# Rotating queries and keys through ScalarE copies, and attention maxima in the projections' PSUM banks, in a two-layer hybrid block

## The chip, the core and the metric

The kernel runs on one core of one Trainium2 chip. The metric is device time in microseconds; the kernel before takes 3040.97 us (median of three runs, 3040.70 to 3048.51). A core has TensorE (PE, with its weight loads listed apart as PEld), VectorE (DVE), ScalarE (ACT), GpSimd (POOL), SyncE (SP) and DMA queues. Each engine executes its own instructions in the order of the program; semaphores order them across engines. Matmuls write to PSUM, 8 banks of 512 fp32 columns per partition; the other engines read the results from there.

## The reference, cut to what matters

Two layers over 512 latent tokens `x` and 256 context tokens `xc`, model width 1024, all in fp32:

```
for l in 0, 1:
    hx, hc = modulated RMS norms of x and xc
    conv, qkv, o, i/f gates, aq, ak, av, branch gates = split(h @ w_in)
    conv_x  = conv branch (GLU, width-31 depthwise conv, layer norm, swish, projection)
    mlstm_x = 4 heads of 256, chunkwise scan forwards and backwards, context first
    q = rope(rms(aq) * q_norm_w);  k = rope(rms(ak) * k_norm_w)    # 8 heads of 64, 2 of keys
    attn_x  = softmax(q @ [k_ctx, k_x]) @ [v_ctx, v_x]
    x = x + g1 * ((gated sum of the three) @ w_out)
    x = x + g2 * conv_ffn(norm(x))
    # layer 0 does the same for xc (its queries see context keys alone, and no rope)
rope(x) = [x1*c - x2*s, x1*s + x2*c]     # halves of 32 channels, c and s per position
```

The norm's factor is one number per token and head, and the rotation mixes only channels of one token and head, so rotation and factor may be applied in either order.

## The kernel before

Channels lie on partitions and tokens on the free axis: a tile is 128 channels by 512 latent and, in layer 0, 256 context tokens (`tq` is 768 in layer 0 and 512 in layer 1). Every fp32 operand is split into a high and a low part, and a product is three matmuls: hl by wh, hh by wl, hh by wh (L717).

Weights stream in units of four 128x128 blocks (256 KB). `Weights.load` issues the DMA of a unit from SP; `Weights.split` makes the high part on ACT (L215) and the low part by a subtraction (L217), on POOL, or on DVE for odd units while `shared` is set; it is set in the output projections and in the down projection at the end of layer 0, where odd units arrive in tiles P of other use. `take` hands out blocks; at the start of a unit it has split `SPLITS` = 2 units ahead.

The order of the work is made when the program is built. A `Filler` holds a queue of projections and runs them step by step (a step is three matmuls of 512 columns, or six, of 512 and 256, in layer 0), and after each step it ticks chains: generators that issue some instructions and then `yield` a number of ticks until the next. Chains touched here are `mgates` (the i/f gates: a serial row of DVE and ACT instructions, L840 to L960, whose table `t` goes to PE at L904), `qk_norm` (L1026: square, norm sums through PE, factor, rotation), `prepare` (L1453: for each of 8 heads, scores' row maxima by blocks of 128 queries; matmuls L1472 and L1479, maxima L1473 and L1481, transposition L1489 into an extra row of the query tile) and the mLSTM heads. The latter follow the tables `HEADS` and `HEADS1`: `2:S0 16:R0` starts the scores of group 0 (three pairs of chunk blocks, L1111, `score_gap` steps apart) at step 2, and its normalisation at step 16; the denominators are summed on DVE at L1131 and go to PE at L584.

PSUM has three pools: `sm` (2 tiles of 512 columns), `pv` (2 of 512) and `mm`, the projections' own, which has 2 tiles of 1024 in layer 0 and 4 of 512 in layer 1. Of the two `pv` tiles one holds the running weighted sum of attention (L1565, read out by L1573) during a head, so the maxima of the next head go through the other, one after the other.

## Time and profile before

| | |
|---|---|
| median of three runs | 3040.97 us (3040.70 to 3048.51) |
| the profiled execution | 3040.4 us, of which the span from first to last instruction 3038.6 us |
| mean granted TensorE clock | 0.973 of full speed |
| PE busy | 2827.8 us, 93% of the span |
| DVE, ACT, POOL busy | 1817.7, 1156.8, 1146.6 us |

The profile is one execution. Its page gives busy time by engine; the view of waits lists, for a stretch, which line of PE waited for which instruction of another engine; the view by windows gives the busy time of each engine in a stretch with the clock granted to TensorE (1 is 2.4 GHz and 0.5 is 1.2 GHz); the timeline gives instructions one by one. Stages by time from the span's start: gates of layer 0 at 61 to 105 us, attention of layer 0 at 740 to 1000, its output projection from 1100, gates of layer 1 at 1805 to 1850, the mLSTM heads of layer 1 at 1850 to 2260, attention at 2300 to 2520, output projection at 2596 to 2700.

### The profile page before, as it was taken

How to read it: one execution, taken by the hardware profiler on the slowest of the kernel's cores; microseconds unless marked ns; L12 is line 12 of the kernel's file. 1: busy time of each engine (PE TensorE's matmuls, PEld its weight loads, DVE VectorE, ACT ScalarE, POOL GpSimd, SP SyncE). 2: the span in 40 equal slices, each digit the busy share in tenths (PEclk: the TensorE clock that was granted, in tenths of full speed). 3: DMA queues.
4: the chain of work that ended last, by engine and by line, in shares of the span. 5: the costliest groups of instructions: out<-in, count | busy, mean ns of one | idle time of the engine just before them, and what ended most of it. 6: DMA issues, size and time to landing. Idle time of an engine off the chain costs nothing. (4 is left out here: it accounts for less than half of the span.)

```text
span 3038.6 us, 42068 instructions
## 1 busy us (share of the span) xinstructions
PE 2827.8 (93%) x15970; PEld 2381.7 (78%) x15970; DVE 1817.7 (60%) x2521; ACT 1156.8 (38%) x2122; POOL 1146.6 (38%) x931
## 2 busy tenths in 40 slices
PE   7999999899889998999999988999889889899999
PEld 4888888787667887888888867887767567778887
DVE  4376787825554336876765555777774763554444
ACT  5224334324345334322322253433444344443333
POOL 2233343224244334333333333333344345444444
PEclk9999999999999999999999999999999999999999
DMA  6454334221010242333333232333322112423333
GB/s 242 133 149 69 58 67 68 49 60 52 28 28 29 63 130 93 115 101 118 118 115 115 75 102 68 65 75 67 65 75 69 39 38 76 154 87 100 93 96 110
DMA packets 156681, 262.47 MB, mean 86 GB/s; under 512 B 17784, under 2 KB 37624, under 8 KB 156480
## 3 DMA queue, kind: packets, MB, share of 16 engines
q1 hardware_dynamic: 142560, 249.67, 28.0%
q10 hardware_dynamic: 13920, 10.12, 3.1%
q8 instruction: 126, 2.06, 0.3%
q14 instruction: 75, 0.61, 0.1%
HBM read 247.05 MB, written 5.46 MB: 83 GB/s over the span
## 5 line engine op out<-in xcount | busy, mean ns | idle before, releaser
L217 POOL TENSOR_TENSOR wl<-raw,wh 128x512 fp32r<-128x512 f32 x659 | 904.6, 1379 | 1507.6 <-ACT wh L215 1461.0
L717 PE MATMUL mm<-hh,wh 128*128 128x512 f32 (+1 forms) x2672 | 963.6, 361 | 17.0 <-DVE big L1619 7.1
L717 PE MATMUL mm<-hh,wl 128*128 128x512 f32 (+1 forms) x2672 | 949.1, 355 | 10.7 <-POOL wl L217 10.6
L717 PE MATMUL mm<-hl,wh 128*128 128x512 f32 (+1 forms) x2672 | 954.4, 357 | 2.1 <-POOL hl L372 1.2
L215 ACT ACTIVATE wh<-raw 128x512 fp32r<-128x512 f32 x662 | 411.2, 625 | 580.2 <-PE mm L717 358.4
L717 PEld LDWEIGHTS mm<-hh,wh 128*128 128x128 f32 x2672 | 512.4, 192 | 113.3 <-issue 29.6
L717 PEld LDWEIGHTS mm<-hh,wl 128*128 128x128 f32 x2672 | 510.4, 191 | 89.4 <-POOL wl L217 15.5
L717 PEld LDWEIGHTS mm<-hl,wh 128*128 128x128 f32 x2672 | 512.3, 192 | 71.4 <-POOL hl L372 1.8
L717 PE MATMUL mm<-C,wh 128*128 128x512 f32 (+1 forms) x1168 | 410.2, 351 | 0.3 <-DVE C L372 0.3
L717 PE MATMUL mm<-B,wh 128*128 128x512 f32 (+1 forms) x976 | 344.4, 353 | 24.4 <-DVE big L1619 11.8
L717 PE MATMUL mm<-B,wl 128*128 128x512 f32 (+1 forms) x976 | 342.5, 351 | 9.2 <-POOL wl L217 8.8
L993 DVE SCALAR_TENSOR_TENSOR AC<-G,par,AC 128x783 f32<-128x783 f32 (+1 forms) x240 | 261.1, 1088 | 3.6
L717 PEld LDWEIGHTS mm<-C,wh 128*128 128x128 f32 x1168 | 226.6, 194 | 28.3 <-DVE C L372 0.5
L717 PEld LDWEIGHTS mm<-B,wh 128*128 128x128 f32 x976 | 190.1, 195 | 53.7 <-ACT wh L215 14.5
L717 PEld LDWEIGHTS mm<-B,wl 128*128 128x128 f32 x976 | 189.4, 194 | 37.4 <-POOL wl L217 14.2
L1669 DVE SCALAR_TENSOR_TENSOR AC<-mm,par,AC 128x511 f32<-128x511 f32 (+1 forms) x132 | 86.7, 656 | 199.0 <-ACT AC L1667 199.0
L1619 DVE SCALAR_TENSOR_TENSOR big<-mm,mod,big 128x512 f32<-128x512 f32 (+1 forms) x144 | 91.1, 657 | 116.3 <-PE mm L717 116.1
L1667 ACT ACTIVATE AC<-mm,par 128x768 f32<-128x768 f32 (+1 forms) x88 | 77.4, 880 | 145.0 <-PE mm L717 144.8
L372 POOL TENSOR_TENSOR P<-t,P 128x512 fp32r<-128x512 f32 (+1 forms) x64 | 75.1, 1175 | 139.2 <-ACT t L1550 111.2
L527 DVE SCALAR_TENSOR_TENSOR P<-C,cs,P 128x512 f32<-128x512 f32 x112 | 116.5, 1072 | 0.9 <-DMA C<-aw 0.9
L1565 PE MATMUL pv<-P,B 128*128 128x512 f32 (+1 forms) x336 | 94.6, 387 | 12.1 <-DVE G L1573 5.2
L1097 ACT ACTIVATE C<-rb,bias 128x128 f32<-128x128 f32 x312 | 96.4, 390 | 21.4 <-DMA rb<-rows 11.2
(282 smaller groups left out, 3726.5 us busy)
## 6 DMA issues: line engine op xcount, KB each, us to landing
raw<-ws SPq DMA_DIRECT2D x662, 256.0 KB, 2.6
C<-aw SPq DMA_DIRECT2D x104, 256.0 KB, 3.0
big<-aw SPq DMA_DIRECT2D x64, 256.0 KB, 4.7
P<-ws SPq DMA_DIRECT2D x30, 256.0 KB, 2.9
big<-xt SPq DMA_DIRECT2D x16, 384.0 KB, 6.3
rb<-rows ACTq DMA_DIRECT2D x40, 128.0 KB, 4.2
den<-rd ACTq DMA_DIRECT2D x40, 64.0 KB, 6.3
den<-rd SPq DMA_DIRECT2D x40, 64.0 KB, 6.3
```

The lines of the kernel that those rows point to most:

```text
L215: self.nc.scalar.activation(out=hi, in_=raw, func=AF.Copy)
L217: eng.tensor_tensor(out=lo, in0=raw, in1=hi.bitcast(F32), op=ALU.subtract)
L372: (eng or dve).tensor_tensor(out=out, in0=src, in1=hi.bitcast(F32), op=ALU.subtract)
L527: dve.scalar_tensor_tensor(out=a_, in0=r_, scalar=cs[:, k, q:q + 1], in1=a_, op0=ALU.mult, op1=ALU.add)
L717: pe.matmul(ps[:, o:o + n], w[w_], h[h_][:, so:so + n], start=(k == 0 and i == 0 and o % 512 == 0), stop=(k == n_k - 1 and i == 2), skip_g ...
L993: dve.scalar_tensor_tensor(out=a, in0=t[:, j:j + cw], scalar=par(l, "cw", w0 + j), in1=a, op0=ALU.mult, op1=ALU.add)
L1097: act.activation(out=t[:, off + x * 128:off + x * 128 + 128], in_=rb[:, c0:c0 + 128], func=AF.Exp, bias=bcol(dr, h, key, qb))
L1565: pe.matmul(o_[:, 0:n_q], vblock(b, a_)[:, 64 * v_:64 * v_ + 128], b_[:, 0:n_q], start=(ki == 0 and x == 0), stop=(last and x == 2))
L1619: dve.scalar_tensor_tensor(out=xs[m][:, o:o + n], in0=ps[:, po:po + n], scalar=gain[:, m, s:s + 1], in1=xs[m][:, o:o + n], op0=ALU.mult, o ...
L1667: act.activation(out=t[:, 0:tq], in_=ps[:, 0:tq], func=AF.Identity, scale=fw(1), bias=fb)
L1669: dve.scalar_tensor_tensor(out=t[:, o + 1:o + n], in0=ps[:, o:o + n - 1], scalar=fw(0), in1=t[:, o + 1:o + n], op0=ALU.mult, op1=ALU.add)
```

## The change

It has four parts. First, `qk_norm` rotates before the norm's factor is known: one tick after the projection's eviction, four copies on ACT swap the halves (32 partitions by 512 columns each), then three DVE products of 128x512 follow; the factor is multiplied in last. Before, the swap and the product with the sine were four DVE products of 32x512 after the factor. Second, `prepare` takes its latent maxima in `mm` tiles: in layer 0 two blocks of 512 columns or four of 256 per tile, and one reduction for the tile; in layer 1 the six reductions stay, one tile each. Context queries stay in `pv`. Third, while `shared` is set the parts of odd units go to tiles AC instead of the ring of `wh` and `wl`, and splits run one unit further ahead. Fourth, `mgates` yields more ticks, 33 in all instead of 21, and the tables move: in layer 1 the first o gate of head 0 runs before the gates' end, `score_gap` is 4 instead of 5 there, R0 stands at 18 instead of 16, S1 at 25 instead of 22, R1 at 41 instead of 39.

```diff
-HEADS1 = [["c o0 o1 q v", "2:S0 4:D1 16:R0 22:S1 39:R1 40:V0 61:V1 61:D*"]] * 3 +     [["c o0 o1 b b x0", "2:S0 4:D1 15:R0 21:S1 35:R1 38:V0 51:V1 51:s"]]
+HEADS1 = [["c o1 q v", "2:S0 4:D1 18:R0 25:S1 41:R1 42:V0 60:V1 60:D*"]] + [["c o0 o1 q v", "2:S0 4:D1 18:R0 25:S1 41:R1 42:V0 61:V1 61:D*"]] * 2 +     [["c o0 o1 b b x0", "2:S0 4:D1 15:R0 21:S1 35:R1 38:V0 51:V1 51:s"]]
...
-       dict(COMMON, partial=3, heads=HEADS1, early=1, first_max=8, send_gap=3, norm_gap=11, first="Q g K v",
+       dict(COMMON, partial=3, score_gap=4, heads=HEADS1, early=1, first_max=8, send_gap=3, norm_gap=11, first="Q g K o v",
...
-            hi = self.pool.tile([128, UNIT * 128], F32R, tag="wh", name=f"wh{self.l}_{u}")
-            lo = self.pool.tile([128, UNIT * 128], F32R, tag="wl", name=f"wl{self.l}_{u}")
+            if self.shared and u % 2:
+                hi, lo = self.room(), self.room()
+            else:
+                hi = self.pool.tile([128, UNIT * 128], F32R, tag="wh", name=f"wh{self.l}_{u}")
+                lo = self.pool.tile([128, UNIT * 128], F32R, tag="wl", name=f"wl{self.l}_{u}")
...
-            self.split(u + SPLITS + 1)
+            self.split(u + SPLITS + 1 + self.shared)
...
-                yield 5
+                yield 6
                 dve.tensor_scalar(out=u[R, :], in0=e[R, :], scalar1=1.0, scalar2=None, op0=ALU.add)

                 dve.scalar_tensor_tensor(out=e[R, :], in0=u[R, :], scalar=1.0, in1=e[R, :], op0=ALU.subtract,
                                          op1=ALU.subtract)
-                yield 1
+                yield 2
                 act.activation(out=ln[R, :], in_=u[R, :], func=AF.Ln)
                 act.activation(out=u[R, :], in_=ln[R, :], func=AF.Exp, scale=-1.0)
                 dve.tensor_tensor(out=e[R, :], in0=e[R, :], in1=u[R, :], op=ALU.mult)
+                yield 3
+                dve.tensor_tensor(out=ln[R, :], in0=ln[R, :], in1=e[R, :], op=ALU.subtract)
                 yield 2
-                dve.tensor_tensor(out=ln[R, :], in0=ln[R, :], in1=e[R, :], op=ALU.subtract)
-                yield 1
                 for P_, nat, sc in dirs:
                     dve.scalar_tensor_tensor(out=lf[P_, sc], in0=z[P_, nat], scalar=0.0, in1=ln[P_, nat], op0=ALU.min,
                                              op1=ALU.subtract)
-                yield 2
+                yield 3
                 dve.tensor_tensor_scan(out=ms[R, :], data0=lf[R, :], data1=li[R, :], initial=NEG, op0=ALU.add, op1=ALU.max)
-                yield 2
+                yield 3
                 dve.tensor_tensor_scan(out=g[R, :], data0=rm[R, :], data1=lf[R, :], initial=0.0, op0=ALU.mult, op1=ALU.add)
-                yield 2
+                yield 3
                 rr, em, be = z, e, u
                 for P_, nat, sc in dirs:
                     dve.tensor_tensor(out=rr[P_, nat], in0=g[P_, sc], in1=ms[P_, sc], op=ALU.subtract)
+                yield 2
                 act.dma_start(out=rdram, in_=rr[R, :])
-                yield 1
+                yield 2
                 for P_, nat, sc in dirs:
...
+                while len(rope) < 2:
+                    rope.append(alloc("rb", 2, 512))
+                    act.dma_start(out=rope[-1], in_=A["rope"][:, len(rope) - 1])
+                yield 1
+                u = t3()
+                for a in range(4):
+                    b = a ^ 1
+                    copy(u[32 * a:32 * a + 32, 0:L], t[32 * b:32 * b + 32, 0:L])
+                dve.tensor_tensor(out=t[:, 0:L], in0=t[:, 0:L], in1=rope[0], op=ALU.mult)
+                dve.tensor_tensor(out=u[:, 0:L], in0=u[:, 0:L], in1=rope[1], op=ALU.mult)
+                dve.tensor_tensor(out=t[:, 0:L], in0=t[:, 0:L], in1=u[:, 0:L], op=ALU.add)
                 yield 3
                 for o, n, s in sts:
                     half_sums(sq, o, n)
-                yield 4
+                yield 6
                 for o, n, s in sts:
                     r = half_spread(sq, o, n)
                     dve.tensor_tensor(out=t[:, o:o + n], in0=t[:, o:o + n], in1=r, op=ALU.mult)
-
-                while len(rope) < 2:
-                    rope.append(alloc("rb", 2, 512))
-                    act.dma_start(out=rope[-1], in_=A["rope"][:, len(rope) - 1])
-                u = t3()
-                for a in range(4):
-                    b = a ^ 1
-                    dve.tensor_tensor(out=u[32 * a:32 * a + 32, 0:L], in0=t[32 * b:32 * b + 32, 0:L],
-                                      in1=rope[1][32 * b:32 * b + 32, :], op=ALU.mult)
-                dve.tensor_tensor(out=t[:, 0:L], in0=t[:, 0:L], in1=rope[0], op=ALU.mult)
-                dve.tensor_tensor(out=t[:, 0:L], in0=t[:, 0:L], in1=u[:, 0:L], op=ALU.add)
...
+                elif what == "o":
+                    fill.add(o_gate(0, 0))
...
-                    if s == 0:
-                        for qb in range(q0, q0 + nb):
-                            ps = pv()
-                            pe.matmul(ps, q1[:, qb * 128:qb * 128 + 128], ks_[v_][:, 0:L], start=True, stop=True)
-                            dve.reduce_max(out=mx[:, qb:qb + 1], in_=ps, axis=AX.X)
-                            yield opt["prep"]
-                    m_ = mc if s == 0 else mx
-                    for qb in range(q0, q0 + nb, 2):
-                        ps = pv()
-                        for j in range(2):
-                            pe.matmul(ps[:, j * C:j * C + C], q1[:, (qb + j) * 128:(qb + j) * 128 + 128], ks_[v_][:, L:T],
-                                      start=(j == 0), stop=True, skip_group_check=True)
-                        dve.reduce_max(out=m_[:, qb:qb + 2], in_=ps.rearrange("p (j n) -> p j n", j=2), axis=AX.X)
-                        if qb + 2 < q0 + nb:
-                            yield opt["prep"]
+
+                    for to, keys_, per in ((mx, slice(0, L), banks[1] // L), (mc, slice(L, T), banks[1] // C)):
+                        if s:
+                            to, per = mx, 2
+                        if s and keys_.start == 0:
+                            continue
+                        nk = keys_.stop - keys_.start
+                        for qb in range(q0, q0 + nb, per):
+                            ps = mm(per * nk) if s == 0 else pv()
+                            for j in range(per):
+                                pe.matmul(ps[:, j * nk:j * nk + nk], q1[:, (qb + j) * 128:(qb + j) * 128 + 128],
+                                          ks_[v_][:, keys_], start=(j * nk % 512 == 0), stop=True, skip_group_check=True)
+                            dve.reduce_max(out=to[:, qb:qb + per], in_=ps[:, 0:per * nk].rearrange("p (j n) -> p j n", j=per),
+                                           axis=AX.X)
+                            if keys_.start == 0 or qb + per < q0 + nb:
+                                yield opt["prep"]
```

On DVE, at the end of the gates of layer 0, this is the row of instructions before (t at L889 is the table that PE waits for at L904; L372 evicts the low part of a projection from its `mm` tile):

```order
L873 TENSOR_TENSOR C_556<-C_562,C_561 4x256
L877 TENSOR_TENSOR C_558<-C_555,C_562 32x512
L877 TENSOR_TENSOR C_558<-C_555,C_562 32x256
L877 TENSOR_TENSOR C_558<-C_555,C_562 4x512
L877 TENSOR_TENSOR C_558<-C_555,C_562 4x256
L884 COPY t_135_759<-C_562 36x5
...
L889 TENSOR_TENSOR t_136_765<-t_135_759,cst 36x120
L372 TENSOR_TENSOR B_790<-mm_693,B_789 128x768
L893 TENSOR_SCALAR C_557<-C_561 32x512
```

In the changed kernel L877 is L883, L884 is L890, L889 is L895 and L372 is L376, and the same place on DVE reads:

```order
L878 TENSOR_TENSOR C_556<-C_562,C_561 4x256
L461 TENSOR_TENSOR mod_95<-sm_813,pre_78 128x16
L376 TENSOR_TENSOR B_858<-mm_775,B_857 128x768
L883 TENSOR_TENSOR C_558<-C_555,C_562 32x512
L883 TENSOR_TENSOR C_558<-C_555,C_562 32x256
L883 TENSOR_TENSOR C_558<-C_555,C_562 4x512
L883 TENSOR_TENSOR C_558<-C_555,C_562 4x256
L890 COPY t_147_865<-C_562 36x5
...
L895 TENSOR_TENSOR t_148_871<-t_147_865,cst 36x120
L899 TENSOR_SCALAR C_557<-C_561 32x512
```

The eviction of the last projection (from mm_775) has moved ahead of the four subtractions and the table; before, the last eviction stood behind the table.

On PE, in the second head of layer 0's attention that follows the first scores, this is before (L1472 is a maximum's matmul, L1544 and L1545 the scores, L717 the projections, L1565 the weighted sum; the brackets name the engines of the semaphores waited for):

```order
L1472 MATMUL pv_679_7467<-B_582_6803,C_669_7426 128x512 [waits DVE_49,Activation_49]
L1544 MATMUL sm_680_7470<-C_597_6913,B_582_6803 128x512
...
L717 MATMUL mm_673_7434<-AC_608_6991,wl0_131_7327 128x256
L1472 MATMUL pv_684_7485<-B_582_6803,C_669_7426 128x512 [waits DVE_49]
L1565 MATMUL pv_674_7441<-P_676_7448,B_579_6796 128x512 [waits Activation_49]
...
L1472 MATMUL pv_689_7500<-B_582_6803,C_669_7426 128x512 [waits DVE_49]
```

And the same place in the changed kernel (L1488 is the maximum's matmul, L721 the projections, L1575 the weighted sum):

```order
L1488 MATMUL mm_673_7460<-B_586_6840,C_663_7419 128x512 [waits PE_49,Activation_49]
L1488 MATMUL mm_673_7460<-B_586_6840,C_663_7419 128x512
...
L721 MATMUL mm_667_7427<-AC_608_6995,wl0_131_7334 128x256
L1488 MATMUL mm_678_7479<-B_586_6840,C_663_7419 128x512 [waits DVE_49]
L1488 MATMUL mm_678_7479<-B_586_6840,C_663_7419 128x512
L1575 MATMUL pv_668_7434<-P_670_7441,B_577_6786 128x512 [waits Activation_49]
...
L1488 MATMUL mm_683_7495<-B_586_6840,C_663_7419 128x256 [waits DVE_49]
```

The maxima have moved from `pv` to `mm`, two blocks side by side; the running projection holds one `mm` tile (mm_667), so the second and the third tile of maxima still wait for DVE, which reads the tile before them.

On ACT, in the output projection of layer 0, this is the row of splits before (unit 193 and 195 are odd; L637 and L680 belong to the norm):

```order
L215 ACTIVATE wh_192_10310<-raw_192_10257 128x512
L215 ACTIVATE wh_193_10334<-raw_193_10280 128x512
L589 ACT_TABLE_LOAD
L589 ACTIVATE t_1133_10304<-sm_10360,eps 128x128
L634 ACTIVATE rs_9978<-big_9962 128x256
L215 ACTIVATE wh_194_10385<-raw_194_10298 128x512
L215 ACTIVATE wh_195_10403<-P_10320 128x512
```

And in the changed kernel, where L215 is L219 and L589 is L593:

```order
L219 ACTIVATE wh_192_10267<-raw_192_10214 128x512
L219 ACTIVATE AC_10271<-raw_193_10237 128x512
L219 ACTIVATE wh_194_10295<-raw_194_10255 128x512
L593 ACT_TABLE_LOAD
L593 ACTIVATE t_1109_10261<-sm_10321,eps 128x128
L638 ACTIVATE rs_9935<-big_9919 128x256
L219 ACTIVATE AC_10346<-P_10281 128x512
```

Odd units now have tiles AC, and the copy of unit 194 has moved ahead of the norm's instructions behind which it stood.

## Rows read from the trace of the kernel before

**Rows 1.** The page: busy time, share of the span and instructions of each engine.

```profile
PE 2827.8 (93%) x15970; PEld 2381.7 (78%) x15970; DVE 1817.7 (60%) x2521; ACT 1156.8 (38%) x2122; POOL 1146.6 (38%) x931
```

**Rows 2.** Windows: us; busy PE, PEld, DVE, ACT, POOL; clock, DMA share, GB/s.

```profile
740.00:1000.00 260.00, 229.69 (x1230) 184.32 (x1230) 147.10 (x204) 125.33 (x237) 103.11 (x88) 0.96 0.11 31
1100.00:1200.00 100.00, 83.91 (x471) 71.33 (x470) 51.66 (x83) 42.57 (x73) 46.25 (x37) 0.93 0.32 99
1850.00:2260.00 410.00, 376.13 (x2227) 324.47 (x2227) 309.39 (x443) 165.98 (x378) 154.72 (x134) 0.96 0.33 69
2300.00:2520.00 220.00, 191.27 (x858) 142.47 (x857) 146.47 (x201) 99.35 (x173) 85.80 (x72) 0.96 0.14 44
2596.00:2700.00 104.00, 88.54 (x589) 78.52 (x588) 62.87 (x107) 47.98 (x89) 41.58 (x34) 0.92 0.40 134
```

**Rows 3.** Windows behind the two waits for the gates' table.

```profile
92.50:102.00 9.50, 9.50 (x35) 8.56 (x36) 2.96 (x15) 2.72 (x5) 1.28 (x1) 0.50 0.34 104
1830.00:1843.00 13.00, 7.29 (x33) 7.22 (x34) 8.45 (x29) 3.47 (x7) 1.32 (x1) 0.50 0.18 49
```

**Rows 4.** Timeline of DVE, rotations in layer 0: start, us, engine, line, out<-in.

```profile
753.48 6.26 DVE L1047 TENSOR_TENSOR t<-G,rb 32x512 f32<-32x512 f32 x4
774.66 1.38 DVE L1047 TENSOR_TENSOR t<-B,rb 32x512 f32<-32x512 f32 x2
```

**Rows 5.** Timeline of POOL beside the first of them.

```profile
755.27 2.25 POOL L372 TENSOR_TENSOR C<-C,AC 128x768 fp32r<-128x768 f32 x1
```

**Rows 6.** Instructions of L366: ns min/median/max, first and last start, forms.

```profile
L366 ACT ACTIVATE den<-pv x50: 257/377/599, 28.5 to 2534.6; 64x256 f32<-64x256 f32 x32, 64x128 f32<-64x128 f32 x16, 128x512 f32<-128x512 f32 x2
```

**Rows 7.** Waits of PE, 740 to 1000: us in total, times, longest.

```profile
PE pv L1472 <- DVE mx L1473: 9.3, 7, 6.6
PE pv L1479 <- DVE G L1573: 4.2, 2, 2.3
```

**Rows 8.** Waits of PE, 2260 to 2520.

```profile
PE pv L1472 <- DVE mx L1473: 14.7, 12, 5.3
```

**Rows 9.** Instructions of L1473.

```profile
L1473 DVE TENSOR_REDUCE mx<-pv x64: 627/684/694, 738.6 to 2498.5; 128x1 f32<-128x512 f32 x64
```

**Rows 10.** Waits of PE, 1000 to 1200.

```profile
PE mm L717 <- POOL wl L217: 8.3, 8, 2.6
PE mm L717 <- ACT wh L215: 4.3, 4, 1.3
```

**Rows 11.** Waits of PE, 2600 to 2710.

```profile
PE mm L717 <- POOL wl L217: 6.9, 12, 1.1
```

**Rows 12.** Waits of PE, 0 to 100.

```profile
PE sm L904 <- DVE t L889: 3.1, 1, 3.1
```

**Rows 13.** Timeline of DVE, end of the gates of layer 0.

```profile
86.98 3.13 DVE L877 TENSOR_TENSOR C<-C,C 32x512 f32<-32x512 f32 x4
92.05 0.28 DVE L889 TENSOR_TENSOR t<-t,cst 36x120 f32<-36x120 f32 x1
92.25 0.94 DVE L372 TENSOR_TENSOR B<-mm,B 128x768 fp32r<-128x768 f32 x1
```

**Rows 14.** Waits of PE, 1700 to 1860.

```profile
PE sm L904 <- DVE t L889: 8.6, 1, 8.6
```

**Rows 15.** Timeline of DVE, gates of layer 1, first and last instruction of the chain.

```profile
1813.86 0.55 DVE L852 TENSOR_SCALAR C<-C 36x768 f32<-36x768 f32 x1 [8.69 <-ACT C L846]
1835.38 0.27 DVE L889 TENSOR_TENSOR t<-t,cst 36x120 f32<-36x120 f32 x1
```

**Rows 16.** Waits of PE, 1860 to 2260.

```profile
PE sm L584 <- DVE den L1131: 23.6, 8, 3.6
```

**Rows 17.** Timeline of PE, two pairs of scores and the normalisation behind.

```profile
1954.93 1.59 PE L1111 MATMUL sm<-B,B 128*128 128x256 f32 x12
1959.79 1.59 PE L1111 MATMUL sm<-B,B 128*128 128x256 f32 x12
1967.24 0.92 PE L584 MATMUL sm<-den,cst 128*32 128x128 f32 x8 [3.11 <-DVE den L1131]
```

More of the change, by code (lines that the diff above doesn't have):

```diff
@@ L188, with __init__ @@
 class Weights:
-    def __init__(self, nc, dram, l, pool, more):
-        self.next, self.shared, self.more = None, False, more
+    def __init__(self, nc, dram, l, pool, more, room):
+        self.next, self.shared, self.more, self.room = None, False, more, room
         self.nc, self.dram, self.l, self.pool = nc, dram, l, pool
@@ L755, in build @@
         more = lambda u: alloc("P", PB, UNIT * 128)
-        W = Weights(nc, A["ws"], 0, wp, more)
+        room = lambda: tac(UNIT * 128, F32R)
+        W = Weights(nc, A["ws"], 0, wp, more, room)
         first = ada_first()
@@ L788, in build @@
             if wc:
-                W.next = Weights(nc, A["ws"], l + 1, wp, more)
+                W.next = Weights(nc, A["ws"], l + 1, wp, more, room)
             plans.append(W.blocks)
@@ L890, in mgates @@
                                   in1=selrow[R].rearrange("p (n o) -> p n o", o=1).to_broadcast([36, 8, 15]), op=ALU.mult)
-                yield 3
+                yield 4
                 for P_, nat, sc in dirs:
@@ L894, in mgates @@
                                       op1=ALU.mult)
-                yield 2
+                yield 3
                 for dr in range(2):
```

6 lines of the change are left out of this document (3 added, 3 removed).

## The prediction

> **What bounds the kernel now.** First the page's busy times: PE is busy for 2827.8 us of a span of 3038.6 [rows 1], so 210.8 us of PE idle time are all that a change which leaves the matmuls alone can win, apart from the clock. DVE, at 60%, is the next. Then the windows, to see where PE idles: attention of layer 0 (260.00 less 229.69, 30.3 us idle), its output projection (16.1 in 100), attention of layer 1 (28.7 in 220) and the output projection of layer 1 (15.5 in 104) [rows 2]. The last number but two of such a row is the granted clock. It has two levels, 1 and 0.5, so a mean of 0.96 over 260 us is 0.08 x 260 = 21 us at the low level. The reader is to see in the windows behind the two gate waits that the clock stands at 0.50 there [rows 3]: PE stood still before, and the time behind a wait is dear too. I count a stretch at the low level as half of its busy time lost: 0.96 in 260 us with PE busy 88% is 9.2 us, 0.96 in 220 is 7.7, 0.93 in 100 is 5.9, 0.92 in 104 is 7.1. Last the waits of each such stretch, which name what came last. None of these stretches is held by one engine at its limit: they are short waits for a DVE, POOL or ACT instruction that was queued too late. So the question for each part is whether the awaited instruction now comes earlier than PE gets there.
>
> **Rotation.** A rotation was four DVE products of 32x512 and two whole instructions; it becomes four ACT copies of 32x512 and three whole instructions. A product is 1.38 / 2 = 0.69 us undisturbed, but four took 6.26 us once [rows 4], while POOL had work on tiles in SBUF beside them [rows 5]. Per rotation DVE is relieved of four products and gains one (the factor is counted in both): three by 0.69, 2.1 us, up to 5.6 where it is disturbed as in that row. There are ten rotations (five per layer), so 21 us or more of DVE, none on PE directly. ACT pays: no row shows a copy of 32x512; the nearest is the copy group of L366, whose longest, that of 512 columns, is 0.60 us [rows 6]. Ten by four by 0.60 are 24 us of an engine busy 38%. What hides them is the ACT idle time of attention (125.33 of 260 busy and 99.35 of 220 [rows 2]). If that cover fails, the exponentials and hi copies behind them are late and PE pays up to 10 us of the 24, at best none; I take 3, near the covered end, since ACT is less than half busy in these rows. The product in place must wait for the copies, so everything queued on DVE behind it (a reduction of a maximum, an eviction) is held for up to 4 x 0.60 = 2.4 us; that is contained in the attention terms.
>
> The stall at 753 to 762 is the place to weigh a rule. The row shows four small products at 1.57 us each beside POOL. The Trainium skill, page "SBUF — State Buffer", section "Who interferes with whom", says that a DVE instruction with two inputs in SBUF contends with a GpSimd instruction that reads there, while ScalarE never waits. The rows above agree with it (6.26 us for four beside POOL, 1.38 for two later). It speaks partly against the change: three whole products with two such inputs stay. By it the worst rotation would go from 6.26 + 1.4 us to 4 x 0.60 + 3 x 1.57 = 7.1 us, and the 6.6 us wait there would hardly shrink, making the layer-0 attention term 7 instead of 10.
>
> **Maxima.** In attention of layer 0 PE waits 9.3 us for the reductions of maxima at L1472 and 4.2 at L1479 because the free `pv` tile is being read out [rows 7]. A head's latent maxima take three `mm` tiles after, six `pv` tiles before. A reduction of 512 columns takes 0.684 us [rows 9]; one of 1024 lies between that and twice, 1.37; I take 1.37, since no row shows a fixed part. The work on DVE then is at best a little less; what changes is the number of places at which PE needs the tile back. Upper bound: both waits and the clock, 13.5 + 9.2 = 22.7. Lower bound: there are two `mm` tiles in layer 0, one of them held by the running projection, so a second tile of maxima waits for the reduction of the first, as the order shows. A wait of that kind cost up to 2.3 us here [rows 7]; at every other of 8 x 3 = 24 tiles that is 27.6 us, a loss of 14. I take a gain of 10: most of the largest wait (6.6) goes with the rotation's shorter hold of DVE, a third of the clock's 9.2 with it, and the rest about cancels. In layer 1 there are four `mm` tiles of which a projection holds one. The 14.7 us in 12 waits [rows 8] were waits of the next maximum for the tile of the last one, and with three free tiles they go, unless DVE itself is behind; upper bound 14.7 + 7.7 = 22.4, lower bound 0, where the reductions (as many as before) are what ends last and PE meets them at the transposition instead. I take half, 11.
>
> **Weights.** In the output projection of layer 0 PE waits 8.3 us for POOL's and 4.3 for ACT's half of a unit, at most 2.6 us each time [rows 10]. A unit is four blocks, a step each, of six matmuls in layer 0; 83.91 us busy for 471 matmuls [rows 2] are 1.07 us a step, so a unit lasts PE 4.3 us. A split one unit further ahead is 4.3 us earlier, more than the longest wait of 2.6, so nearly all of these go if the raw unit is there: DMA is at a share of 0.32 and 0.40 [rows 2]. Upper bound 12.6 + 5.9 = 18.5, lower bound 3 (tiles AC, of which there are four and a unit takes two, come free late), taken 8. In layer 1 the same kind of wait is 6.9 us, at most 1.1 [rows 11]; upper 6.9 + 7.1 = 14.0, lower 3, taken 7.
>
> **Gates.** In layer 0 PE waits 3.1 us for the table [rows 12]. There DVE starts L877 at 86.98 and ends L889 at 92.05 + 0.28 = 92.33: 5.35 us, followed after by the eviction of 0.94 [rows 13]. In the changed order the eviction of the last query-key projection goes first, and between that projection's end and L910 PE has only 18 matmuls of 256 columns, some 2.2 us. So PE waits about 0.3 + 0.94 + 5.35 + some 0.5 for the sum's other rows, less 2.2: 4.9. That is 1.8 more; I take a loss of 2 (from 4 lost, the clock held low longer, to 3 won, if DVE is ahead of this). In layer 1 the wait is 8.6 us [rows 14], at the end of a DVE row that begins at 1813.86 and ends at 1835.38 + 0.27, 21.8 us almost without a gap [rows 15]. The o gate's eight steps of 0.69 (below) are 5.5 us and stand ahead of the wait, so about 3 us stay. The longer yields can hold the row back only if the ticks run out before DVE does. Lower 0, upper 5.5 + 3.6 (half of the 7.29 busy us at the low clock [rows 3]) = 9.1, taken 5, because a wait of 3.1 was enough for the low clock in layer 0.
>
> **Heads of layer 1.** PE waits 23.6 us in eight places for the denominators, at most 3.6 [rows 16]: two per head. Two pairs of scores start 4.86 us apart, with a pair (1.43) and five steps between: 0.69 a step. The last pair before ends about 1961.2, the normalisation starts at 1967.24 after four steps and 3.11 us of wait [rows 17]. With score_gap 4 and R0 at 18, the order has eight steps there in heads 0 to 2 (before: four), in the last head five (before: three); R1 has eight or nine, before seven. So R0's waits lose up to 4 x 0.69 = 2.8 us in three heads and 1.4 in one, R1's 0.7 to 1.4 in four: 9.8 + 4 at best, 14. Against this the pairs come 0.69 us sooner while DVE, busy 309.39 of 410 us here [rows 2], is still on the pair before: lower 2. I take 7, the middle.
>
> **The sum.** 10 + 11 + 8 + 7 - 2 + 5 + 7 - 3 = 43 us. The profiled execution took 3040.4 us, 0.6 under the median, so 2997.4 there and 2998 for a median.
>
> **Rivals.**
> First, the slots in layer 0 take the attention gain back: its term is -5 and that of layer 1, where DVE is the limit, 5. Sum 22, 3019 us. For it speaks that the order has waits on DVE at the second and third tile of maxima; against it that three tiles replace six. 0.15.
>
> Second, the waits only move on. DVE is busy 146.47 of 220 us in attention of layer 1 [rows 2]; if it ends last there and in the heads, those terms are 0 and 2, the gates' 0, that of layer 0's attention 7: 17, so 3024 us. Against it: with 73 us of idle time DVE isn't full. 0.10.
>
> Third, the other side: slower. A rotation now holds DVE's queue until four ACT copies are done, and ACT's queue has exponentials and splits before them. The reductions stand behind it on DVE, and now they hold `mm` tiles, so a projection's next block cannot start: a stop of the very stream that fills PE, where before only the maxima stopped. Price: 2.3 us a tile [rows 7]; at 16 of the 24 tiles of layer 0 that is 37 us, with layer 1's new waits set against the old ones that go in both layers. The other terms, 8 + 7 - 2 + 5 + 7 - 3, give 22 back: 15 us slower, 3056 us. It decides from the point at which 14 tiles wait so long (14 x 2.3 less 22 is the 0.3% named below). Against it: the reductions' input needs no rotation that isn't long done, and there are only five rotations in a layer. 0.08.
>
> Fourth, it doesn't do what it says: the AC tiles come free no sooner than the ring did, and the table arrives as late as now, so the weights' 15 and the gates' 5 fall away: 23, so 3018 us. 0.05.
>
> My forecast has 0.62. A difference of 0.3%, 9 us, is about what a measurement of this kernel can tell. Faster than 3031.9 us is nearly all of the forecast, most of the first and the fourth rival and three quarters of the second: 0.84. Within: 0.08; slower: 0.08. All terms at their lower ends would be 3060 us, all at their upper ends some 2937; the range of eight in ten is 2962 to 3032, and the forecast's own 2975 to 3015.
>
> **What would show it.** Rotation: no DVE group of 32x512 left, and no PE wait above 4 us in 740 to 1000. Maxima: waits at L1488 under 5 us in layer 1's attention. Weights: less than 5 us of waits on L219 and L221 per output projection, the clock 0.97 or more. Gates: the wait at L910 about 5 us in layer 0 and 3 in layer 1. Heads: the sum at L588 below 14 us. The forecast is wrong if waits on reductions at L721 or L1488 in layer 0 add up to 20 us, or if those at L1575 or L1499 grow by what L1488 loses.

## The result and the profile after

The changed kernel takes 3005.33 us (median of four runs, 3001.07 to 3006.52), against 3044.74 for the kernel before beside it: ratio 0.9865, 95% interval 0.9839 to 0.9890. Repeated later, beside the experiments e9 and e10, it is 0.9878 (0.9864 to 0.9891). The forecast of 2998 in a range of 2962 to 3032 held. The profiled execution has a span of 3003.2 us, 35.4 less than before.

The page's line of busy times answers to [rows 1]: the same matmuls, DVE down by 32.0 us, ACT up by 19.2.

```profile
PE 2816.8 (94%) x15970; PEld 2378.2 (79%) x15970; DVE 1785.7 (59%) x2467; ACT 1176.0 (39%) x2158; POOL 1152.1 (38%) x931
```

The windows of the same stages in the changed kernel, columns as in [rows 2]:

```profile
740.00:985.00 245.00, 229.14 (x1258) 186.87 (x1257) 139.22 (x171) 129.89 (x246) 105.72 (x89) 0.98 0.11 34
1083.00:1183.00 100.00, 87.10 (x489) 74.16 (x490) 52.51 (x86) 44.08 (x75) 46.16 (x37) 0.93 0.31 99
1823.00:2243.00 420.00, 378.66 (x2260) 326.29 (x2260) 301.65 (x440) 168.75 (x387) 153.95 (x134) 0.96 0.32 67
2283.00:2488.00 205.00, 185.04 (x857) 140.33 (x856) 138.48 (x189) 107.16 (x187) 87.69 (x72) 0.97 0.16 47
```

Layer-0 attention idles 15.9 us where it idled 30.3, and its clock went from 0.96 to 0.98. The heads of layer 1 idle 41.3 us in 420, more than the 33.9 in 410 before.

Windows of different length are hard to compare, so I set stages against each other by progress. The marks are the times at which the n-th matmul of the projection and value lines ends; the same n is the same point of the program in every kernel. The table gives the gain of a stage against the kernel before, and PE's idle time in it (the sum of its gaps), in us. The last five columns are experiments below; where two numbers stand, they are two profiles. Everything is set against one profile of the kernel before.

| stage (n) | forecast | changed | no ACT rotation (e1, e10) | old maxima (e2) | maxima alone (e5) | maxima and splits (e9) | old splits (e4) |
|---|---|---|---|---|---|---|---|
| to 113 us, gates of layer 0 (300) | -2 | 0.6, -0.4 | 0.6, 0.0 | -0.1 | -0.4 | 3.5 | 0.2 |
| heads of layer 0 (3100) | 0 | -2.9, -3.4 | -3.9, -4.2 | -4.0 | -5.9 | -2.9 | -2.9 |
| attention, layer 0 (3900) | 10 | 19.9, 19.9 | 21.0, 22.0 | 3.9 | 21.7 | 20.9 | 19.7 |
| output projection, layer 0 (4900) | 8 | 3.1, 3.3 | 3.7, 4.9 | 3.4 | -0.9 | 4.8 | -0.9 |
| feed-forward, layer 0 (8050) | 0 | 1.4, 2.6 | 4.2, 2.1 | 0.7 | 0.4 | 0.9 | 0.9 |
| gates and heads, layer 1 (9700) | 12 | -5.1, -6.9 | -1.3, -1.7 | -4.5 | 1.6 | -5.2 | -1.4 |
| attention, layer 1 (10700) | 11 | 13.6, 13.2 | 16.2, 15.7 | -0.6 | 16.0 | 16.2 | 12.7 |
| output projection, layer 1 (11100) | 7 | 5.2, 5.1 | 2.0, 3.2 | 5.0 | 0.2 | 3.1 | 1.9 |
| idle: attention, layer 0 (before 30.2) | | 15.9, 15.8 | 15.7, 15.6 | 28.2 | 15.8 | 15.8 | 15.7 |
| idle: gates and heads, layer 1 (before 40.3) | | 45.0, 44.7 | 41.9, 43.7 | 43.3 | 40.1 | 39.8 | 43.7 |
| idle: attention, layer 1 (before 32.8) | | 23.9, 24.3 | 21.8, 21.5 | 33.8 | 22.1 | 21.5 | 23.8 |

The forecast's -3 for ACT's copies was put in no stage and isn't in the column. The clock scatters a stage by some 4 us, and more in the gates and heads of layer 1. The maxima alone change nothing in the heads of layer 0 and show -5.9 there, with idle time of 23.4 instead of 21.8 and 17 us at the low clock level instead of 7. In the gates and heads of layer 1, e5 and e9 have the same tables of steps as before and idle times of 40.1 and 39.8, and yet gains of 1.6 and -5.2: the low level took 44 us in one and 65 in the other. So a difference of a few us in one stage of one profile shows little by itself; I lean on the waits and on whole runs.

**Attention.** PE's waits in layer-0 attention, which answer to [rows 7], are now

```profile
PE mm L1488 <- DVE mx L1490: 4.1, 9, 1.2
PE sm L609 <- DVE B L1057: 2.6, 1, 2.6
PE pv L1499 <- DVE mx L1495: 2.1, 1, 2.1
PE mm L721 <- DVE mx L1490: 1.8, 2, 0.9
PE sm L609 <- DVE G L1057: 1.6, 1, 1.6
```

The new waits on a maximum's tile are nine of 0.5 us each, not of 2.3, and projections wait 1.8 us in two. Before, these lines stood there too:

```profile
PE pv L1565 <- DVE G L1573: 4.4, 2, 2.2
PE pv L1565 <- DVE B L1573: 2.2, 1, 2.2
PE pv L1479 <- DVE B L1573: 1.9, 1, 1.9
PE pv L1479 <- DVE mx L1473: 1.4, 4, 0.8
```

The first three and the 4.2 us of [rows 7] are 12.7 us in which PE waited for the instruction that reads out the running weighted sum. All of these are gone in the changed kernel, where the latent maxima no longer stand in `pv`, and in e5; in e2, with the maxima back in `pv`, all 12.7 us are back. That is most of the 14 us of idle time won in this stage, and the prediction counted only 4.2 of it. In layer 1 the first three lines, to be set against [rows 8], are

```profile
PE pv L1499 <- DVE mx L1495: 9.2, 6, 4.1
PE mm L721 <- DVE mx L1490: 3.1, 1, 3.1
PE mm L1488 <- DVE mx L1490: 2.0, 1, 2.0
```

so of 14.7 us at the maxima 2.0 stay, and 9.2 stand at the transposition behind them, where the lower bound of that term had put them. Before, the transposition took

```profile
PE pv L1489 <- DVE mx L1485: 3.1, 4, 0.9
```

and without the ACT copies it takes 3.2 (e1, below), while e2, with the copies and without the move, has 6.8. So the move of the maxima did not bring these waits; they came with the copies.

**The rotation.** DVE's timeline around a rotation in layer 0:

```profile
746.84 0.69 DVE L1048 TENSOR_TENSOR G<-G,rb 128x512 f32<-128x512 f32 x1 [3.85 <-ACT t L370]
747.45 0.68 DVE L1049 TENSOR_TENSOR t<-t,rb 128x512 f32<-128x512 f32 x1
748.17 1.67 DVE L1050 TENSOR_TENSOR G<-G,t 128x512 f32<-128x512 f32 x1
749.75 1.21 DVE L1490 TENSOR_REDUCE mc<-mm 128x4 f32<-128x1024 f32 x1
```

and ACT's and POOL's beside it:

```profile
744.26 2.55 ACT L370 ACTIVATE t<-G 32x512 f32<-32x512 f32 x4
```

```profile
747.54 1.75 POOL L221 TENSOR_TENSOR wl<-raw,wh 128x512 fp32r<-128x512 f32 x1 [2.75 <-ACT wh L219]
```

Four copies take 2.55 us (2.4 forecast). DVE stands still for 3.85 us until they are done, and a reduction of a maximum in an `mm` tile stands behind. The sum after them takes 1.67 us beside POOL's subtraction, the product before it 0.68, though it overlaps with POOL as well. The Trainium skill, page "SBUF — State Buffer", section "Who interferes with whom", says that a DVE instruction with two inputs in SBUF contends with a GpSimd instruction that reads there; the row of the sum agrees. A reduction of 1024 columns takes 1.21 us, not twice 0.684 [rows 9]. By the Trainium skill, page "VectorE: DVE Perf Modes", section "The TRN2 errata — SBUF-src ops pay a fixed extra latency per instruction", an estimate from its row for PSUM is (120 + 1024) / 0.96 GHz = 1.19 us; the measured row agrees.

This stop in layer 0 cost PE little by itself: the stage idles as long with the copies (15.9, 15.8) as without (15.7, 15.6). In layer 1 the two longest waits at the transposition, 2.4 and 4.1 us, each stand behind such a stop. The second:

```profile
2353.23 0.69 DVE L1048 TENSOR_TENSOR rs<-rs,rb 128x512 f32<-128x512 f32 x1 [2.87 <-ACT t L370]
2361.04 0.38 PE L1499 MATMUL pv<-cst,mx 128*4 128x128 f32 x2 [4.13 <-DVE mx L1495]
```

### The profile page after: what moved, and what is told of

It reads as the page before. It is cut to its first block, busy times and chain, and to the rows that moved or that the text cites. A ratio compares the mean times of both kernels' runs of the same rounds, so it can differ in the third digit from the quotient of the medians.

```text
span 3003.2 us, 41997 instructions
## 1 busy us (share of the span) xinstructions
PE 2816.8 (94%) x15970; PEld 2378.2 (79%) x15970; DVE 1785.7 (59%) x2467; ACT 1176.0 (39%) x2158; POOL 1152.1 (38%) x931
## 5 line engine op out<-in xcount | busy, mean ns | idle before, releaser
L721 PE MATMUL mm<-hh,wh 128*128 128x512 f32 (+1 forms) x2664 | 961.1, 361 | 21.8 <-DVE big L1629 7.4
L721 PE MATMUL mm<-hh,wl 128*128 128x512 f32 (+1 forms) x2664 | 945.8, 355 | 14.3 <-POOL wl L221 14.2
L721 PE MATMUL mm<-hl,wh 128*128 128x512 f32 (+1 forms) x2664 | 950.8, 357 | 2.1 <-POOL hl L376 1.2
L219 ACT ACTIVATE wh<-raw 128x512 fp32r<-128x512 f32 x659 | 409.5, 625 | 586.4 <-PE mm L721 332.1
L721 PEld LDWEIGHTS mm<-hh,wh 128*128 128x128 f32 x2664 | 511.3, 192 | 121.1 <-issue 31.3
L721 PEld LDWEIGHTS mm<-hh,wl 128*128 128x128 f32 x2664 | 509.0, 191 | 93.6 <-POOL wl L221 20.4
L721 PEld LDWEIGHTS mm<-hl,wh 128*128 128x128 f32 x2664 | 511.2, 192 | 70.4 <-POOL hl L376 1.8
L721 PE MATMUL mm<-C,wh 128*128 128x512 f32 (+1 forms) x1068 | 378.8, 355 | 0.3 <-DVE C L376 0.3
L721 PE MATMUL mm<-B,wh 128*128 128x512 f32 (+1 forms) x876 | 312.7, 357 | 17.4 <-DVE big L1629 10.0
L721 PE MATMUL mm<-B,wl 128*128 128x512 f32 (+1 forms) x876 | 310.1, 354 | 5.3 <-POOL wl L221 5.1
L721 PEld LDWEIGHTS mm<-C,wh 128*128 128x128 f32 x1068 | 204.0, 191 | 28.4 <-DVE C L376 0.5
L721 PEld LDWEIGHTS mm<-B,wh 128*128 128x128 f32 x876 | 167.6, 191 | 46.3 <-issue 8.8
L721 PEld LDWEIGHTS mm<-B,wl 128*128 128x128 f32 x876 | 167.6, 191 | 31.2 <-POOL wl L221 8.4
L1629 DVE SCALAR_TENSOR_TENSOR big<-mm,mod,big 128x512 f32<-128x512 f32 (+1 forms) x144 | 90.9, 656 | 114.7 <-PE mm L721 114.5
L376 POOL TENSOR_TENSOR P<-t,P 128x512 fp32r<-128x512 f32 (+1 forms) x64 | 75.2, 1176 | 117.8 <-ACT t L1560 91.9
L1189 PE MATMUL pv<-P,C 128*128 128x256 f32 x624 | 96.8, 292 | 7.3 <-DVE P L376 4.6
```

Of the source, the lines that this page charges most:

```text
L219: self.nc.scalar.activation(out=hi, in_=raw, func=AF.Copy)
L376: (eng or dve).tensor_tensor(out=out, in0=src, in1=hi.bitcast(F32), op=ALU.subtract)
L721: pe.matmul(ps[:, o:o + n], w[w_], h[h_][:, so:so + n], start=(k == 0 and i == 0 and o % 512 == 0), stop=(k == n_k - 1 and i == 2), skip_g ...
L1189: pe.matmul(ps[:, dd * 256:dd * 256 + 256], v_[key // 3][:, vo:vo + 128], b_, start=(ki == 0 and i == 0 and dd == 0), stop=(ki == len(part ...
L1629: dve.scalar_tensor_tensor(out=xs[m][:, o:o + n], in0=ps[:, po:po + n], scalar=gain[:, m, s:s + 1], in1=xs[m][:, o:o + n], op0=ALU.mult, o ...
```

## Experiments

**Undo the rotation (e1), and again (e10).** Edit, in the changed kernel:

```diff
-                    copy(u[32 * a:32 * a + 32, 0:L], t[32 * b:32 * b + 32, 0:L])
+                    dve.tensor_tensor(out=u[32 * a:32 * a + 32, 0:L], in0=t[32 * b:32 * b + 32, 0:L],
+                                      in1=rope[1][32 * b:32 * b + 32, :], op=ALU.mult)
...
```

with the order, ticks and tables of before.

> The changed kernel with the rotation of before (four DVE products of 32x512 behind the norm's factor, yields 3 and 4); all else as changed. The changed kernel took 3005.3 us. Theory A, rotation and maxima each give about half of the 20 us won in layer-0 attention and little of that of layer 1: 3005 + 10 = 3015 us, with a PE wait of over 4 us back near 755 us. Rival B, the maxima's move alone makes the gain, since a stall on DVE only reached PE through the single free pv tile: within 3 us of 3005.

> The changed kernel with the rotation of before, again, beside the changed kernel itself on the same chip. Theory A, the rotation through ACT gains nothing, since neither attention stage moved without it: within 5 us of the changed kernel, or better than it. Rival B, the better ratio seen before (0.9845 against 0.9865) was the clock's scatter, and the rotation gains its 2 us times ten behind it: the changed kernel is some 10 us faster.

Measured: 2998.95 us, ratio 0.9845 (0.9831 to 0.9860), and 2999.46 us, 0.9847 (0.9833 to 0.9860), where the changed kernel beside it took 3007.80, 0.9878 (0.9864 to 0.9891). Both attention stages keep their whole gain without the ACT copies. Beside each other (e11 and e10), the kernel with them is 8.3 us slower, though DVE is busy 1785.7 us in it and 1814.2 in e1. In layer 1's attention the waits of e1 are

```profile
PE mm L1487 <- DVE mx L1489: 4.8, 2, 4.0
PE pv L1498 <- DVE mx L1494: 3.2, 5, 1.0
```

8.0 us against the changed kernel's 11.2 at the same two lines, which has 3.1 at a projection besides. In layer 0 the disturbed rotation of [rows 4] is back, and the wait over 4 us that theory A named came with it:

```profile
758.26 6.37 DVE L1053 TENSOR_TENSOR t<-G,rb 32x512 f32<-32x512 f32 x4
766.74 0.58 PE L1498 MATMUL pv<-cst,mx 128*2 128x128 f32 x2 [5.10 <-DVE mx L1489]
```

The 6.6 us wait of before is thus still there without the copies, with 5.1 us and at the transposition. The copies do take it away; in its place PE waits 2.6 and 1.6 us at L609 for the factor's products, queued behind the rotations, and 2.1 at L1499 (the list above), so the stage's idle time stays. Theory A's time, 10 us slower, did not come. Rival B of the first run held, that the maxima alone make the gain, but not its number: the kernel is better, not equal. In e10 theory A held and rival B didn't.

Where do the 8.3 us stand? These are the busy times of e1:

```profile
PE 2808.3 (94%) x15970; PEld 2370.3 (79%) x15970; DVE 1814.2 (61%) x2497; ACT 1155.4 (39%) x2122; POOL 1152.4 (38%) x931
```

The matmuls are the same, and PE is busy for 2816.8 and 2815.7 us in the two profiles with the copies, for 2808.3 and 2811.7 in the two without. Its idle time, span less busy time, is 186.4 and 189.5 with them, 187.9 and 185.4 without. So most of the 8.3 us is not waiting but slower matmuls, at a mean granted clock of 0.975 in both profiles with the copies and of 0.979 and 0.977 without. In attention of layer 1 the copies cost some 2.5 us of idle time, as the waits show. Why the clock was lower with them no run here shows.

**Undo the maxima (e2), or make them alone (e5).** Edit: `prepare` of before in the changed kernel, and the changed `prepare` in the kernel before.

```diff
-                            ps = mm(per * nk) if s == 0 else pv()
+                            ps = pv()
...
```

> The changed kernel with prepare of before (maxima in the one free pv tile); rotation and all else as changed. Theory A: 15 us of layer-1 attention go and half of the 20 of layer 0, so 3005 + 25 = 3030 us, with 12 to 18 us of waits on the reductions between the layer-1 heads. Rival B, the rotation makes the gain because it freed DVE of 20 us: 3005 + 5 = 3010.

> The kernel before with one part of the change alone: prepare takes its latent maxima in the projections' mm tiles. Theory A, the maxima make nearly all of the gain and need no help from the rotation: 16 us in layer-0 attention and 14 in layer 1, ratio 0.990 to the kernel before (some 31 us less). Rival B, they need the DVE time that the rotation frees, and alone meet a DVE that is late: less than 15 us, ratio over 0.995.

Measured: e2 3032.79 us, 0.9956 (0.9944 to 0.9967); e5 3011.47, 0.9890 (0.9875 to 0.9905). Theory A held twice, and stronger than put: without the maxima's move 16 of the 19.9 us in layer 0 and all of layer 1's go. The waits in layer 1 of e2:

```profile
PE pv L1481 <- DVE mx L1482: 17.0, 13, 3.9
PE pv L1498 <- DVE mx L1494: 6.8, 4, 4.2
```

DVE has the rotation's time free there and the waits are longer than in [rows 8]. In layer 1 the part changes only the pool, with as many reductions as before, so what bound there was the one free tile. In layer 0 it also puts two blocks into a tile and halves the tiles; no run separates that from the change of pool. It did not work by relieving DVE, which in e5 is busy 1818.4 us, in the kernel before 1817.7.

**Undo the splits (e4).**

```diff
-            self.split(u + SPLITS + 1 + self.shared)
+            self.split(u + SPLITS + 1)
...
```

with `wh` and `wl` for all units.

> The changed kernel with the splits of before (ring of wh and wl for all units, two units ahead). Theory A: the output projections lose again the 3 us of layer 0 and the 5 of layer 1 that they won, 3005 + 8 = 3013 us, waits on the splits' line 12 us in layer 0 and 10 in layer 1. Rival B, these stages gained from what stands before them (the clock, the order of the norm's work), not from the lead: 3005, waits as in the changed kernel (6.3 and 6.7 us).

Measured: 3011.36 us, 0.9890 (0.9875 to 0.9905). The interval overlaps that of the changed kernel, so the whole run alone would not settle it; by stages theory A holds. The gains of the two output projections go (3.1 to -0.9, 5.2 to 1.9). Waits in layer 0 with the old splits, and then in the changed kernel:

```profile
PE mm L718 <- POOL wl L218: 9.1, 10, 2.6
PE mm L718 <- ACT wh L216: 4.9, 4, 1.9
```

```profile
PE mm L721 <- DVE big L1629: 4.5, 4, 2.8
PE mm L721 <- POOL wl L221: 3.9, 5, 1.1
PE mm L721 <- ACT wh L219: 2.4, 2, 1.8
```

The lead takes 7.7 us of waits away and 4.5 come back at the residual's sum (L1629), the next thing that PE met: 3 of the 8 forecast remain. In layer 1 the waits on the splits are 11.5 us with the old ones and 6.7 in the changed kernel.

**The gates' ticks (e6).** Edit: the old yields in `mgates`, the o gate still first.

> The changed kernel with the ticks of mgates of before (21 instead of 33); the o gate stays ahead of the gates' end. Theory A, DVE's row sets the end of the gates, and the longer yields only delayed it: the wait at L910 of layer 1 falls from 5.4 to about 3 us, that of layer 0 from 3.9 to 3.1; ratio some 0.001 better than the changed kernel's 0.9865. Rival B, the longer yields let evictions pass between the row's instructions and so keep the projections fed: 3 to 6 us more waits at L721 before the gates' end, and the ratio 0.988.

Measured: 3005.99 us, 0.9878 (0.9861 to 0.9895), no difference to the changed kernel in time. The waits of PE for the table, layer 1, changed kernel and e6:

```profile
PE sm L910 <- DVE t L895: 5.4, 1, 5.4
```

```profile
PE sm L909 <- DVE t L894: 8.0, 1, 8.0
```

In layer 0 it is 3.1 with the old yields and 3.9 with the new. Theory A is wrong in layer 1 and right in layer 0. The longer waits at L721 that rival B named didn't come either (11.0 us before the gates' end in layer 1, against 10.6 in the changed kernel). With the old ticks, 12 of the o gate's 24 matmuls and none of the values' stand ahead of L909 in PE's order; with the new ones all 24 and 18 of the values'. So PE comes later, but DVE's row has grown: in the changed kernel it begins and ends at

```profile
1791.78 0.55 DVE L857 TENSOR_SCALAR C<-C 36x768 f32<-36x768 f32 x1 [8.68 <-ACT C L851]
1798.02 1.01 DVE L376 TENSOR_TENSOR B<-mm,B 128x512 fp32r<-128x512 f32 x2
1805.49 0.99 DVE L376 TENSOR_TENSOR B<-mm,B 128x512 fp32r<-128x512 f32 x2
1815.38 0.28 DVE L895 TENSOR_TENSOR t<-t,cst 36x120 f32<-36x120 f32 x1
```

23.9 us instead of 21.8 [rows 15], with two groups of evictions in it instead of one, and longer subtractions: the four of L883 take 3.11 us, and 2.04 in e6, where the row again takes 21.8 us.

**The heads of layer 1 (e3, e7, e8, e12).** Edits, in this order: the old step numbers with score_gap 5; R1 at 44; R0 at 16 and R1 at 43; every second tap of layer 1's convolution left out.

```diff
-HEADS1 = [["c o1 q v", "2:S0 4:D1 18:R0 25:S1 41:R1 42:V0 60:V1 60:D*"]] + ...
+HEADS1 = [["c o1 q v", "2:S0 4:D1 16:R0 22:S1 39:R1 40:V0 61:V1 61:D*"]] + ...
...
+HEADS1 = [["c o1 q v", "2:S0 4:D1 18:R0 25:S1 44:R1 45:V0 61:V1 61:D*"]] + ...
...
+HEADS1 = [["c o1 q v", "2:S0 4:D1 16:R0 25:S1 43:R1 44:V0 60:V1 60:D*"]] + ...
...
+                    if l and j % 2:
+                        return
```

> The changed kernel with layer 1's score_gap 5 and the step numbers of HEADS1 of before (R0 16, S1 22, R1 39), the o gate still ahead of the gates' end. Theory A, the new step numbers brought the 8 us that the heads of layer 1 lost, for the splits on POOL now stand behind the additions of a normalisation: 3005 - 8 = 2997 us, waits at L588 back at 23 us in 8 and none of POOL's 7.2. Rival B, what costs is the o gate that head 0 lacks, or the rotation's copies: then the 7.2 us on POOL stay and waits at R0 come back, 3005 + 6 = 3011.

> The changed kernel with R1 at step 44 and V0 at 45 instead of 41 and 42 in the first three heads of layer 1. Theory A, a normalisation waits because DVE has the six products of the group before and the last pair's sums behind them, a fixed 11 us from the products' start: three steps of 0.69 later, the three waits of 3.2 to 3.5 us at L588 shrink by 2.1 each, 6 us in all. Rival B, the time goes into other waits of the same chain (V0 and V1, the splits on POOL): the sum of idle time of the heads stays within 2 us of 45.

> The changed kernel with R0 back at 16, S1 at 25, R1 at 43 and V0 at 44 in the first three heads of layer 1, so that the products of group 0 (14 steps after R0) come at step 30, before the second pair of S1 (29) has been drained and three steps ahead of the third (33). Theory A: R0's waits come back by two steps, 1.4 us in two or three heads, while R1's, 13 steps after the products instead of 9, lose all of their 3.2 to 3.5: some 6 us less. Rival B, the third pair's own sums bind R1, not the products: R1 two steps later wins 1.4 us a head, and with R0's loss nothing comes of it.

> The changed kernel with every second tap of the depthwise convolution of layer 1 left out (15 of 31 per 128 channels, 60 DVE instructions of about 0.98 us, 59 us of DVE time; that part of the result is left out). The matmuls are the same. Theory A, in the heads of layer 1 PE waits for DVE's queue, and 45 us of idle time only moved from line to line as the tables changed: with 59 us taken from that queue the idle time of the heads falls to below 25 us. Rival B, they are waits for a chain of latencies (PE, DVE, DMA and back), which the taps only fill: idle time stays above 38 us.

Measured: e3 3004.22 us, 0.9863 (0.9848 to 0.9879); e7 3004.59, 0.9870 (0.9854 to 0.9886); e8 3013.86, 0.9896 (0.9879 to 0.9912); e12 3003.43, 0.9861 (0.9843 to 0.9879). PE's idle time in gates and heads is 40.8, 44.6, 47.3 and 42.9 us, where the changed kernel has 45.0 and the kernel before 40.3. The longest waits of the changed kernel, e3, e7 and e12 in this stage:

```profile
PE sm L588 <- DVE den L1138: 19.4, 6, 5.0
PE mm L721 <- POOL wl L221: 7.2, 6, 2.0
```

```profile
PE sm L588 <- DVE den L1138: 24.3, 8, 3.8
```

```profile
PE pv L1189 <- DVE P L376: 12.4, 5, 3.0
PE sm L588 <- DVE den L1138: 12.1, 8, 3.7
```

```profile
PE sm L588 <- DVE den L1140: 19.0, 7, 3.6
```

With the old numbers POOL's 7.2 us are gone and L588 has its 24.3 back: the first half of e3's theory A held, its gain didn't come. In e7 the waits at L588 fell by 7.3 us, as theory A had it, and 9.4 us more came at L1189 (3.0 in the changed kernel): rival B. e8 fits neither: L588 has 25.1 us, and it is 9.3 us slower than e7 beside it. In e12 DVE is busy 58.6 us less and the waits didn't move (POOL's at L721 are 7.0 us), so theory A of that run, a full DVE queue, is refuted. The idle time fits its rival, a chain of latencies, which the taps only fill; that it is such a chain is argued, for no run shortened a link of it. That no edit of steps brought less idle time than the old table (40.8 in e3, 40.3 before) is measured; which link sets it was not isolated.

**Two parts only (e9), and the changed kernel again (e11).** Edit: in the kernel before, the changed `prepare` and `Weights`, nothing else.

```diff
+                            ps = mm(per * nk) if s == 0 else pv()
...
+                hi, lo = self.room(), self.room()
...
+            self.split(u + SPLITS + 1 + self.shared)
```

> The kernel before with two parts of the change: maxima in mm tiles, and the splits (tiles AC for odd units, one unit further ahead). Rotation, gates and heads are those of before. Theory A, these two are all that gains: 32 us of the maxima alone and some 4 each in the two output projections, and nothing is lost in the heads: 40 us under the kernel before, ratio 0.987 to 0.985, at least as good as the whole change. Rival B, the rest of the change is worth something (the gates' wait, 3 us, and the rotation's 20 us of DVE): ratio over 0.988 and 5 us behind the whole change.

> The changed kernel itself, as the measure for the two beside it. Both theories: a ratio of 0.984 to 0.989 to the kernel before; its stages within 4 us of those of its first profile, except where the clock's low stretches fall otherwise.

Measured: e9 2998.70 us, 0.9844 (0.9830 to 0.9857), e11 3007.80, 0.9878 (0.9864 to 0.9891). Two of the four parts are 9.1 us better than all four: theory A, but for its "nothing is lost in the heads", where the stage shows -5.2 us at the clock named above. e10, beside it, is e9 with the gates' ticks and the new tables added, and takes 2999.46 us. So gates and tables together are worth nothing that can be measured, and the whole 9 us go with the rotation. Against e5 (3011.47 us, 0.9890), e9 adds the splits and is 12.8 us faster; the intervals don't overlap.

## Why the prediction was right, point by point

The time was right within 8 us, but by terms that erred both ways, and in that it was luck. By whole runs the maxima gave 32 us where 21 were forecast (e5), the splits 13 for 15 (e9 against e5), the rotation cost 8 for 3 (e10), and the gates and heads gave nothing for 10 (e9 against e10).

- Maxima: 10 + 11 forecast, 19.9 + 13.6 measured, and e5 shows 21.7 + 16.0 for this part alone. The mechanism was right and its size wrong, in two steps. One is the price of a new wait: 0.5 us at nine places, where 2.3 had been taken for the lower bound. That 2.3 was a wait for the weighted sum's reader (L1573), not for a reduction; apart from the 6.6 the waits of [rows 7] for a reduction took 2.7 us in six, and those of L1479 for one 1.4 in four. The other is that only 4.2 of the 12.7 us of waits for L1573 were counted. In layer 0 14.3 us came from idle time, 5 from the clock (the stage spent 10.2 us at the low level instead of 20.5). I had credited the rotation with the largest wait (6.6 us). The copies do take it away, but others come in its place, and in e5, where it stays with 5.1 us, the stage gains as much.
- Rotation: "none on PE directly" and 3 us for ACT was on the good side; it costs 8 us, inside the 10 that the prediction allowed. What failed is the use of the relief of DVE, which was true (28.5 us by the page) and worth nothing. DVE's stops for the copies, of 2.9 to 3.9 us at six rotations of the attention stages, are seen in PE's waits in layer 1 (some 2.5 us of idle time); the rest of the 8 came with a lower clock and is not traced to them. The rule of the Trainium skill's page "SBUF — State Buffer", section "Who interferes with whom", had been weighed for the worst rotation, and the 1.67 us row bears it out.
- Weights: 8 + 7 forecast, 3.1 + 5.2 measured. The step "nearly all of these go" held for half of the splits' waits in layer 0 (12.6 to 6.3), and what was late next was left out: 4.5 us at the residual. In layer 1 the prediction counted POOL's 6.9 us and not ACT's 4.1 beside them; of the 11.0, 6.7 stay. The stage's idle time fell by 1.7 us there, and the time at the low clock level from 10.2 to 3.7, so most of that gain is the clock's.
- Gates: layer 0 -2 forecast, 0.6 and -0.4 measured; the wait is 3.9 (4.9 forecast, 3.1 before). Layer 1's wait fell to 5.4 instead of 3. Missing in that step: evictions moved ahead of the table, as seen in layer 0 but not priced in layer 1, where DVE's row grew by 2.1 us. In time e6 finds no gain in the ticks.
- Heads: 7 forecast, none gained: idle time of gates and heads went from 40.3 to 45.0, though the gates' wait won 3.2, so the heads' own grew by 8. In whole runs this loss doesn't show (e3, and e9 against e10). The step for R0 held: its four waits fell from 10.4 to 4.1 us in all. R1's rose from 13.2 to 15.3; the step that failed counted R1's distance from the last pair. In DVE's timeline of the changed kernel

```profile
1868.50 3.98 DVE L1164 TENSOR_TENSOR C<-C,den 128x512 f32<-128x512 f32 x6
1872.41 0.94 DVE L999 SCALAR_TENSOR_TENSOR AC<-G,par,AC 128x512 f32<-128x512 f32 x1
1873.27 1.14 DVE L1131 SCALAR_TENSOR_TENSOR C<-sm,C 128x256 f32<-128x256 f32 x4
1874.34 1.10 DVE L1138 TENSOR_TENSOR den<-C,C 128x512 f32<-128x512 f32 x1
1875.47 3.96 DVE L1138 TENSOR_TENSOR den<-den,C 128x256 f32<-128x256 f32 x4
```

R1's sums stand behind the six products of group 0, which come 14 steps after R0 and moved with it: 9 steps before R1 in both tables. e7, with 12 steps between, has shorter waits at L588, which fits; e8, with 13, has longer ones, which doesn't, so this link is not settled. Beside them POOL and then PE do

```profile
1869.27 0.85 POOL L1166 TENSOR_TENSOR C<-C 128x256 f32<-128x256 f32 x1 [6.00 <-DVE C L1164]
1872.09 1.57 POOL L1169 TENSOR_TENSOR C<-C 128x128 f32<-128x128 f32 x2 [0.49 <-DVE C L1164]
1873.63 4.34 POOL L221 TENSOR_TENSOR wl<-raw,wh 128x512 fp32r<-128x512 f32 x3
1874.94 0.50 PE L721 MATMUL mm<-hh,wl 128*128 128x512 f32 x1 [2.00 <-POOL wl L221]
```

splits queued behind additions that wait for DVE, hence the 7.2 us at L721, which no term held.

Of the rivals none came as it was written. The first's waits are there and small. The waits that the second has move on stand in part at the transposition of layer 1 (9.2 us). Its sum is off: its terms, with -2 left for the gates of layer 0, add up to 19 and not 17, so 3022 us. The third's mechanism, DVE held by ACT's copies, is there in layer 1; all that goes with the copies is 8 us, not 37. The fourth's splits did come sooner, and so did the table in layer 1.

Of the signs named ahead, those of the rotation and the maxima came (no wait above 2.6 us in layer-0 attention, 2.0 at L1488 in layer 1). Those of the weights did not: 6.3 and 6.7 us of waits on the splits, at clocks of 0.93 and 0.92. The gates' waits were 3.9 and 5.4 for "about 5" and 3, and the sum at L588 was 19.4 for "below 14". The sign of a wrong forecast at L1499 came by half: it grew by 6.1 us where L1488 lost 12.7.

## What to carry to other kernels

A wait for an engine can be a wait for the tile that the engine reads: look at how many buffers of that pool are free, and what else uses it, before relieving the engine. Here other PSUM tiles were worth 32 us (e5), while 28 us of DVE time, bought with copies on ACT, gained nothing and 58.6 us in the heads (e12) moved no wait. Moving work to an idle engine adds a hand-over in an in-order queue, so price what stands behind it. A step that is moved takes its followers with it, so look for the instruction that binds before counting steps. And a sum that comes out right can hide terms that don't: undo the parts one by one.

## What was not expected of the hardware

The 1024-column reduction from PSUM at 1.21 us against 0.684 for 512: 0.16 us less than two of these. A table of steps that cuts 7.3 us of waits at one line and leaves the stage's idle time at 44.6 (45.0 before). And 58.6 us of DVE work taken out of layer 1 for 2.1 us less idle time in its heads.
